# Hybrid decoder layer on one core: head transfers issued by ScalarE, no filler products among the first transposes, and two scans tied behind low parts

## The chip, the cores and the metric

The kernel runs on one core of one Trainium2 chip. The core has five engines that run side by side and meet at semaphores: TensorE (PE in the profile, with PEld for its weight loads), VectorE (DVE), ScalarE (ACT), GpSimd (POOL) and SyncE (SP), which here only issues transfers. The metric is the device time of one execution in microseconds (us); lower is better. Three runs of the kernel before gave 948.83, 948.57 and 948.82 us, median 948.82 us.

## The reference

One decoder layer works on 1024 tokens of width 1024, ahead of which 16 learned meta tokens are put, so 1040 rows:

```
u = rmsnorm(h, g_pre_mix)
q, k, v, xr, yr = split(u @ w_in)
attn = sliding_window_attention_with_sinks(q, k, v, sinks)
xr = causal_depthwise_conv(xr, conv_w, conv_b)
hr = rg_lru(xr, w_a, b_a, w_x, b_x, lambda)      # h[t] = a[t]*h[t-1] + u[t]
rec = gelu(yr) * hr
h = h + rmsnorm(concat(attn, rec) @ w_out, g_post_mix)
u = rmsnorm(h, g_pre_ffn)
h = h + rmsnorm(relu(u @ w_ff1)**2 @ w_ff2, g_post_ffn)
```

Everything is float32. The output is the last 1024 rows.

## The kernel before, in words

Every float32 operand of a large product is split into a high part (a copy rounded to fp32r, made by ScalarE) and a low part (the operand minus the high part, made by VectorE). A product is then three matmuls, high by high (line 125), high by low (line 130) and low by high (line 131); the function `mm3` issues them. So each operand has two producers, and TensorE needs both. A matmul that finds its low part unfinished stops TensorE, which takes its instructions in order.

The kernel is written in a framework that plans the order. The program text gives each instruction a priority by its place; the planner then runs a simulated timeline with its own costs and puts the instructions of each engine into one fixed queue. On the chip each engine works through its queue strictly in order, waiting where an input is not there. The text can force an order within an engine with `behind(name, ins)`, which makes no semaphore and only tells the planner that `ins` stands after `name`. `chained(0, ins)` and `chained(1, ins)` use the same means to string the instructions of ScalarE and of VectorE behind each other in the head.

**The head** (lines 138 to 530). SP issues the meta tokens (line 142), the first two tiles of 128 input rows (`load_x`, line 147), the two norm weights `g_pre_mix` and `g_pre_ffn` (lines 155, 156) and then the weights of k, v and q, the other row tiles between them (`fetch`, line 384). The norm weights land in 16 rows of `vmt`, are turned by a TensorE transpose (line 160) into the bank `pg` and copied to `gcol` (line 161), one column for each of eight groups of 128 features.

TensorE meanwhile multiplies zeros by zeros (`load`, line 309): 12 products of 512 columns and 6 of 256 stand in front of its first real work. They write a bank that nobody reads.

The first three row tiles are normed at once: meta by `norm_rows` (Square on ScalarE at line 254, the root on GpSimd at lines 170 and 176, the scaling on VectorE at line 260), the first two full tiles by `norm_first` (Square on ScalarE at line 237, for the first tile half of it on VectorE at line 242; root on ScalarE at line 82; reciprocal on VectorE at line 199; scaling in two halves at line 248). Then `transposed` turns the eight groups kc of 128 features: for each kc three transposes, of meta, tile 0 and tile 1, into one of six banks (line 358), one product of zeros behind them (line 365), the scaling by `gcol` with rounding on ScalarE (line 117) and the low part on VectorE (line 118). Two casts that make the high part of the key weight (line 344) go between the first scalings of ScalarE. The products of k and v (line 282, function `part`) start on the scaled groups. The remaining rows follow in three more pieces, each with transposes and products.

**The recurrent stage** (lines 798 to 981). The recurrent width of 512 is four chunks c of 128. For each chunk, after the gates, `decay(c)` makes the decay factor and a tanh on ScalarE, and `recur(c)` a square root on ScalarE and three VectorE instructions: lines 871 and 872, which make the input of the recurrence, and line 873, `tensor_tensor_scan`, which runs it over 1040 steps. `rec_out(c, half)` multiplies the result by the gelu branch (line 878) and splits it.

**The output projection.** `w_out` comes in eight groups kc of 128 rows. `load_wo` and `split_wo` bring and split them; their low parts are line 99 with output tag `a`, from a buffer `raw` or `d`. Groups 0 to 3 belong to the attention half; 4 and 5 meet chunks 0 and 1 of the recurrence, 6 and 7 chunks 2 and 3. `out_mm` takes groups 0 to 3 for the first four row tiles (banks pt, o, acc, s), then groups 4 and 5 for all four, then 6 and 7. The rest of the kernel, from about 260 us on, is the feed-forward part.

Of the kernel before, what the change touches and what calls it, by code (L numbers as in the profile page):

```python
# [10 lines left out]
F32R = mybir.dt.float32r  # L11
AF = mybir.ActivationFunctionType
ALU = mybir.AluOpType
# [3 lines left out]
P = 128  # L17
# [3 lines left out]
NMETA = 16  # L21
# [16 lines left out]
def hybrid_layer(  # L38
# [6 lines left out]
    nc = tc.nc  # L45
# [33 lines left out]
    last_lut = [None]  # L79
# [58 lines left out]
    ident = const.tile([P, P], F32, name="ident")  # L138
    make_identity(nc, ident)

    meta_t = slot("d", [NMETA, D])
    nc.sync.dma_start(meta_t, meta_tokens)
    xt = []

    def load_x(i):
# [6 lines left out]

    vmt = const.tile([P, P], F32, name="vmt")
    g_r = vmt[0:16, :]
    nc.sync.dma_start(g_r[0:8, :], g_pre_mix.rearrange("o (k p) -> (o k) p", p=P))
    nc.sync.dma_start(g_r[8:16, :], g_pre_ffn.rearrange("o (k p) -> (o k) p", p=P))

    gcol = const.tile([P, 16], F32, name="gcol")
    pg = bank("o")
    nc.tensor.transpose(pg[:, :16], g_r, ident[:16, :16])  # L160
    nc.vector.tensor_copy(gcol, pg[:, :16])
    g_mix_col, g_ffn_col = gcol[:, 0:8], gcol[:, 8:16]

    half_pow = const.tile([P, 1], F32, name="half_pow")
# [19 lines left out]
    eps_col = const.tile([P, 1], F32, name="eps_col")  # L184
# [7 lines left out]

    load_root()

    def root_rstd(ssq, bias, n=P):
        sd = small.tile([P, 1], F32, name="sd", tag="sd")
        lut(sd[:n], ssq, AF.Sqrt, bias=bias)
        rs = small.tile([P, 1], F32, name="rs", tag="rs")
        nc.vector.reciprocal(rs[:n], sd[:n])
        return rs[:n]  # L200


# [29 lines left out]
    def norm_first(src, halves):  # L232

        xn = slot("d", [P, D])
        ss = [small.tile([P, 1], F32, name=f"hq{i}", tag=f"hq{i}") for i in range(2)]
        c = slice(0, 512 if halves else D)
        nc.scalar.activation(
            xn[:, c], src[:, c], AF.Square, scale=RMS_SC, accum_out=ss[0]
        )
        if halves:  # L240
            c = slice(512, D)
            nc.vector.tensor_tensor_reduce(
                out=xn[:, c], in0=src[:, c], in1=src[:, c], scale=RMS_SC * RMS_SC,
                scalar=EPS, op0=ALU.mult, op1=ALU.add, accum_out=ss[1],
            )
        rs = root_rstd(ss[0], ss[1] if halves else eps_col)
        for c in (slice(0, 512), slice(512, D)):
            nc.vector.tensor_scalar(xn[:, c], src[:, c], rs, None, op0=ALU.mult)
        return xn

    def norm_rows(src, n, link=False):
        xn = slot("d", [P, D])
        ssq = small.tile([P, 1], F32, name="ssq", tag="ssq")
        ins = nc.scalar.activation(
            xn[:n], src, AF.Square, scale=RMS_SC, accum_out=ssq[:n]
        ).ins
        if link:
            chained(0, ins)
        rs = rstd_of([ssq[:n]], n)
        ins = nc.vector.tensor_scalar(xn[:n], src, rs, None, op0=ALU.mult).ins  # L260
        if link:
            chained(1, ins)
        return xn
# [35 lines left out]

    zeros = slot("ws", [P, 512], F32R)  # L300
    nc.vector.memset(f32(zeros), 0.0)

    flip = [0]

# [2 lines left out]
    def load(n, cols, after=None):  # L307
        for _ in range(n):
            ins = nc.tensor.matmul(
                idle[:, :cols], zeros[:, :P], zeros[:, :cols], start=True, stop=True,  # L310
                skip_group_check=True,
            ).ins
            if after:
                behind(after, ins)
        return ins.name

    load(12, 512)
    load(6, 256)

    def normed(b):  # L320
        if b == 0:
            return [
                (norm_rows(meta_t[:NMETA], NMETA), NMETA),
                (norm_first(xt[0], True), P), (norm_first(xt[1], False), P),
            ]
        rows = [(xt[2 * b], P), (xt[2 * b + 1], P)]
        return [(norm_rows(s[:m], m), m) for s, m in rows]


    last = [None, None]  # L330
# [1 line left out]
    def chained(e, ins):  # L332
        if last[e] is not None:
            behind(last[e], ins)
        last[e] = ins.name
# [15 lines left out]
    def transposed(b, xn, after=None):  # L351
        t0, n = ALL[b]
        for kc in range(KC):
            flip[0] += 1
            pt = bank(("pt", "o", "s")[flip[0] % 3])
            o = 0
            for s, m in xn:
                ins = nc.tensor.transpose(
                    pt[:, o : o + m], s[:m, kc * P : (kc + 1) * P], ident[:m, :m]
                )  # L360
                if after:
                    behind(after, ins.ins)
                o += m
            if b == 0:
                load(1, P, ins.ins.name)
            uh, ul = u[kc]
            if b == 0 and kc in (0, 1):
                key_casts.pop(0)()
            high = split_scaled(
                uh[:, t0 : t0 + n], ul[:, t0 : t0 + n], pt[:, :n],  # L370
                g_mix_col[:, kc : kc + 1],
            )
            if b == 0:
                chained(0, high[0])
                chained(1, high[1])
# [17 lines left out]
    xn = normed(0)  # L393
# [14 lines left out]
    low_w(wv, rv)  # L408
    wq = high_w(rq)
    low_w(wq, rq)  # L410
    km = slot("ws", [P, 4, 2 * P], F32R)
    nc.gpsimd.memset(f32(km[:, 0:2, 0 : P - NMETA]), 0.0)
    nc.gpsimd.memset(f32(km[:, 2:4, :]), 0.0)
    nsink = const.tile([P, 8], F32, name="nsink")
    nc.sync.dma_start(nsink, attn_sinks[0].partition_broadcast(P))
    prm_r = slot("d", [8, 512])
# [82 lines left out]
    for b in range(4):  # L499
# [3 lines left out]
        if b == 0:  # L503
# [5 lines left out]
            xn = [(norm_rows(xt[2], P, True), P)]  # L509
# [21 lines left out]
    for h in range(2):  # L531
        r, o, m = HALF[h], HALF[1 - h], slice(P - NMETA, 2 * P)
# [276 lines left out]
    rg = [None] * NLRU  # L809
# [48 lines left out]
    av = [None] * NLRU  # L858

    def decay(c, after=None):  # L860
        r = rg[c][0]
        av[c] = slot("b", [P, TT])
        lut(av[c], r, AF.Exp, scale=m8sp[:, c : c + 1])
        ins = lut(r, r, AF.Tanh, scale=m4sp[:, c : c + 1])
        if after:
            behind(after, ins)

    def recur(c):
        r, gi = rg[c]
        lut(r, r, AF.Sqrt, scale=-1.0)  # L870
        nc.vector.scalar_tensor_tensor(r, av[c], 1.0, r, op0=ALU.add, op1=ALU.mult)
        nc.vector.tensor_tensor(gi, gi, r, op=ALU.mult)
        nc.vector.tensor_tensor_scan(r, av[c], gi, 0.0, op0=ALU.mult, op1=ALU.add)

    def rec_out(c, half, eng=None):
        o = 512 * half
# [23 lines left out]
    def split_wo(kc, tag, eng=None):  # L900
        wo[kc] = pair(tag, [P, D])
        split(wo[kc][0], wo[kc][1], wo_raw[kc], eng)
# [45 lines left out]
        decay(c)  # L948
    for c in (0, 1):
        recur(c)  # L950
    load_wo(0, "raw")
    load_wo(1, "raw")
    load_wo(2, "d")
# [3 lines left out]
    for kc in range(1, 4):  # L957
        split_wo(kc, "a")
        wo_cast[kc] = cast[0]
    decay(2, wo_cast[1])  # L960
    decay(3, wo_cast[2])
    for c in (2, 3):
        recur(c)
    for half in range(2):
        for c in range(NLRU):
            y = ys[c][:, 512 * half : 512 * half + 512]
            ins = lut(y, y, AF.Gelu_apprx_tanh)
            if half == 0 and c == 0:
                behind(wo_cast[3], ins)
    for c0 in (0, 2):  # L970
        at[0][2 + c0 // 2] = pair("b", [P, 2, 512])
        for c in (c0, c0 + 1):
            rec_out(c, 0)
            rec_low = mark[0]
        for kc in range(4 + c0, 6 + c0):
            load_wo(kc, ("d", "raw")[kc % 2])
            split_wo(kc, "a")
    for cp in (2, 3):
        at[1][cp] = pair("b", [P, 2, 512])
    for c in range(NLRU):  # L980
# [487 lines left out]
    halves = {}  # L1468
# [159 lines left out]
```

## Time and profile before

| what | us |
|---|---|
| median of three runs | 948.82 |
| the profiled execution | 949.06 |
| its span, first to last instruction | 947.4 |
| PE busy | 936.9 |
| DVE busy | 664.3 |
| ACT busy | 504.3 |
| POOL busy | 133.9 |

A row of the timeline gives the start in us from the span's start, the duration, the engine, the line of the kernel, the operation, what it writes and reads with shapes, how many such instructions were merged, and in brackets how long the engine had stood idle and what released it. SPq, ACTq and POOLq are the queues of those engines that issue transfers. Matmuls overlap, so a matmul's duration is longer than its distance to the next one; the distance of starts is the cost in a full queue.

### The profile page before, as it was taken

What the parts mean: (1) busy time and instruction counts of PE and PEld (TensorE: products, weight loads), DVE (VectorE), ACT (ScalarE), POOL (GpSimd) and SP (SyncE); (2) the same over time, 40 slices, a digit from 0 to 9 for tenths busy, and PEclk for the clock granted to TensorE, in tenths of its full rate; (3) what the DMA queues carried; (4) which work ended last, traced back from release to release, by engine and by line L of the source; (5) the groups of instructions that cost most, each with busy time, mean ns of one, the idle gap of its engine ahead of it and who ended that gap; (6) DMA issues with size and microseconds to landing.
All of it is one profiled execution on the core that took longest, in us unless ns stands there. A gap on an engine that the chain in (4) does not pass through costs nothing.

```text
span 947.4 us, 12177 instructions
## 1 busy us (share of the span) xinstructions
PE 936.9 (99%) x4584; PEld 783.6 (83%) x4584; DVE 664.3 (70%) x848; ACT 504.3 (53%) x845; POOL 133.9 (14%) x205
## 2 busy tenths in 40 slices
PE   9999999999999999999999999999999999999996
PEld 8999999877788878888888888888888888888885
DVE  6667788889877987665544465476667676779883
ACT  8546765679434664443655575654533443445441
POOL 4104436430021200010000000001111000001201
PEclk9999999999999999999999999999999999999999
DMA  8220011104359659574422364334877756637924
GB/s 273 57 66 25 24 46 45 45 23 140 102 176 271 200 182 285 187 256 134 156 89 89 111 214 121 108 112 112 199 168 176 211 178 194 186 131 209 239 63 89
DMA packets 97366, 134.91 MB, mean 142 GB/s; under 512 B 22230, under 2 KB 61158, under 8 KB 97308
## 3 DMA queue, kind: packets, MB, share of 16 engines
q1 hardware_dynamic: 87996, 108.64, 36.2%
q0 software_dynamic: 8880, 24.19, 12.2%
q10 hardware_dynamic: 432, 1.31, 0.4%
q8 instruction: 36, 0.59, 0.3%
q14 instruction: 22, 0.18, 0.1%
HBM read 112.55 MB, written 20.97 MB: 141 GB/s over the span
## 4 chain that ended last, share of the span: by engine, by line
PE 94%; DVE 3%; issue 1%; DMA 1%; ACT 0%; DVEq 0%; SPq 0%
PE ps_acc L125 11%; PE ps_acc L131 11%; PE ps_acc L130 11%; PE ps_pt L131 6%; PE ps_pt L130 6%; PE ps_pt L125 6%; PE ps_s L125 6%; PE ps_s L131 6%; PE ps_s L130 6%; PE ps_o L125 5%; PE ps_o L130 5%; PE ps_o L131 5%; PE ps_o L699 2%; PE ps_acc L917 1%; PE ps_acc L282 1%
## 5 line engine op out<-in xcount | busy, mean ns | idle before, releaser
L99 DVE TENSOR_TENSOR ws<-raw,ws 128x1024 fp32r<-128x1024 f32 (+1 forms) x69 | 83.1, 1204 | 69.9 <-PE ps_o L130 23.0
L96 ACT CAST ws<-raw 128x1024 fp32r<-128x1024 f32 (+1 forms) x68 | 69.8, 1027 | 82.3 <-PE ps_o L130 33.1
L96 ACT CAST ws<-e 128x1024 fp32r<-128x1024 f32 x41 | 43.0, 1049 | 85.5 <-PE ps_o L130 38.3
L99 DVE TENSOR_TENSOR b<-b,b 128x1024 fp32r<-128x1024 f32 (+1 forms) x49 | 57.5, 1176 | 27.8 <-PE ps_o L130 22.5
L130 PE MATMUL ps_acc<-a,ws 128*128 128x512 f32 (+3 forms) x224 | 76.3, 341 | 0.0
L125 PE MATMUL ps_acc<-a,ws 128*128 128x512 f32 (+3 forms) x224 | 76.3, 341 | 0.0
L131 PE MATMUL ps_acc<-a,ws 128*128 128x512 f32 (+3 forms) x224 | 75.7, 338 | 0.0
L99 DVE TENSOR_TENSOR ws<-e,ws 128x1024 fp32r<-128x1024 f32 x41 | 50.1, 1222 | 31.8 <-ACT ws L96 18.5
L96 ACT CAST b<-b 128x1024 fp32r<-128x1024 f32 (+1 forms) x49 | 49.5, 1011 | 41.7 <-DVE b L1096 35.6
L686 POOL TENSOR_SCALAR_AFFINE_SELECT c<-c 128x512 fp32r<-128x512 f32 x64 | 53.2, 846 | 73.6 <-ACT c L96 64.6
L131 PE MATMUL ps_acc<-ws,b 128*128 128x512 f32 (+1 forms) x120 | 46.1, 384 | 0.0
L130 PE MATMUL ps_acc<-ws,b 128*128 128x512 f32 (+1 forms) x120 | 46.1, 384 | 0.0
L125 PE MATMUL ps_acc<-ws,b 128*128 128x512 f32 (+1 forms) x120 | 46.0, 385 | 0.0
L125 PEld LDWEIGHTS ps_acc<-a,ws 128*128 128x128 f32 x224 | 42.2, 188 | 3.1 <-DVE b L926 0.3
L131 PEld LDWEIGHTS ps_acc<-a,ws 128*128 128x128 f32 x224 | 42.2, 188 | 3.0
L130 PEld LDWEIGHTS ps_acc<-a,ws 128*128 128x128 f32 x224 | 42.1, 188 | 2.8
L125 PE MATMUL ps_pt<-ws,b 128*128 128x512 f32 x112 | 44.3, 395 | 0.0
L130 PE MATMUL ps_pt<-ws,b 128*128 128x512 f32 x112 | 44.2, 395 | 0.0
L131 PE MATMUL ps_pt<-ws,b 128*128 128x512 f32 x112 | 44.0, 392 | 0.0
L125 PE MATMUL ps_s<-ws,b 128*128 128x512 f32 x110 | 43.4, 395 | 0.0
L130 PE MATMUL ps_s<-ws,b 128*128 128x512 f32 x110 | 43.3, 393 | 0.0
L131 PE MATMUL ps_s<-ws,b 128*128 128x512 f32 x110 | 43.2, 393 | 0.0
(421 smaller groups left out, 2682.3 us busy)
## 6 DMA issues: line engine op xcount, KB each, us to landing
raw<-in_w_ff_dram SPq DMA_DIRECT2D x59, 512.0 KB, 3.8
e<-in_w_ff_dram SPq DMA_DIRECT2D x43, 512.0 KB, 3.5
a<-in_w_ff_dram SPq DMA_DIRECT2D x12, 512.0 KB, 6.2
s_dram<-a POOLq DMA_DIRECT2D x12, 512.0 KB, 3.8
raw<-in_w_in_dram SPq DMA_DIRECT2D x9, 512.0 KB, 3.7
c<-in_x_dram SPq DMA_DIRECT2D x8, 512.0 KB, 5.1
d<-in_x_dram SPq DMA_DIRECT2D x8, 512.0 KB, 3.4
out_dram<-raw SPq DMA_DIRECT2D x8, 512.0 KB
```

The lines of the kernel that those rows point to most:

```text
L96: cast[0] = nc.scalar.copy(hi, src).ins.name
L99: low = nc.vector.tensor_tensor(lo, src, f32(hi), op=ALU.subtract).ins
L125: ins = nc.tensor.matmul(dst, lh, rh, start=start, stop=False, skip_group_check=True).ins
L130: nc.tensor.matmul(dst, lh, rl, start=False, stop=False, skip_group_check=True)
L131: last_mm[0] = nc.tensor.matmul(dst, ll, rh, start=False, stop=stop, skip_group_check=True).ins.name
L282: last_mm[0] = nc.tensor.matmul(acc[:, :n], w[k // 2][:, kc, :], u[kc][k % 2][:, t0 : t0 + n], start=k == 0 and kc == 0, stop=k == last an ...
L686: nc.gpsimd.affine_select(out=p_[:, :, s], in_=f32(p_[:, :, 0]), pattern=[[0, 4], [g, P]], compare_op=op, fill=0.0, base=0, channel_multip ...
L699: nc.tensor.matmul(two[:, :, oc : oc + w], v, p_.rearrange("p (j i) s c -> p j (i s c)", j=2)[:, :, pc : pc + w], start=n == 0 and k == 0, ...
L917: ins = nc.tensor.matmul(y2_bank[half], (wh, wh, wl)[k][:, kc, :], (uh, ul, uh)[k][:, t0 : t0 + n], start=m % 24 == 0, stop=m % 24 == 23, ...
```

## The change

1. The issue of the meta tokens and of the two norm weights moves from SP to ScalarE.
2. The transpose of the norm weights moves from the head of TensorE's queue to between the products of zeros: 8 products of 512 columns, the transpose, 4 more of 512 and 4 of 256 (before: 12 of 512 and 6 of 256). Its copy to `gcol` moves into `norm_first` of the first tile, ahead of the reciprocal.
3. The eight products of zeros among the first transposes go away.
4. Orders are tied: the Square of tile 1 behind the last ScalarE table function, its reciprocal behind the scaling of tile 0, and the norms of the third piece into the chains of ScalarE and VectorE.
5. The second cast of the key weight moves from group 1 to group 2 of the features.
6. The zeros for the key block of the meta tokens (`km`) are written in the text before the first transposes.
7. The scan leaves `recur` and becomes a function of its own. The scan of chunk 0 follows both `recur(0)` and `recur(1)`; that of chunk 1 is tied behind the low part of group 2 of `w_out`; that of chunk 2 follows both `recur(2)` and `recur(3)`; that of chunk 3 is tied behind the low part of group 5 of `w_out` and that of `rec_out(1, 0)`.

```
-    nc.sync.dma_start(meta_t, meta_tokens)
+    nc.scalar.dma_start(meta_t, meta_tokens)
...
-    nc.sync.dma_start(g_r[0:8, :], g_pre_mix.rearrange("o (k p) -> (o k) p", p=P))
-    nc.sync.dma_start(g_r[8:16, :], g_pre_ffn.rearrange("o (k p) -> (o k) p", p=P))
+    nc.scalar.dma_start(g_r[0:8, :], g_pre_mix.rearrange("o (k p) -> (o k) p", p=P))
+    nc.scalar.dma_start(g_r[8:16, :], g_pre_ffn.rearrange("o (k p) -> (o k) p", p=P))
...
-    pg = bank("o")
-    nc.tensor.transpose(pg[:, :16], g_r, ident[:16, :16])
-    nc.vector.tensor_copy(gcol, pg[:, :16])
...
-        nc.vector.reciprocal(rs[:n], sd[:n])
+        ins = nc.vector.reciprocal(rs[:n], sd[:n]).ins
+        if after:
+            behind(after, ins)
...
+        if not halves:
+            behind(last_lut[0], square)
...
+            nc.vector.tensor_copy(gcol, pg[:, :16])
+        rs = root_rstd(ss[0], ss[1] if halves else eps_col, after=scaled[0])
...
+    km = slot("ws", [P, 4, 2 * P], F32R)
+    nc.gpsimd.memset(f32(km[:, 0:2, 0 : P - NMETA]), 0.0)
+    nc.gpsimd.memset(f32(km[:, 2:4, :]), 0.0)
...
-    load(12, 512)
-    load(6, 256)
+    pg = bank("o")
+    turned = nc.tensor.transpose(pg[:, :16], g_r, ident[:16, :16]).ins
+    behind(load(8, 512), turned)
+    load(4, 512, turned.name)
+    load(4, 256)
...
-        return [(norm_rows(s[:m], m), m) for s, m in rows]
+        return [(norm_rows(s[:m], m, b == 2), m) for s, m in rows]
...
-            if b == 0:
-                load(1, P, ins.ins.name)
...
-            if b == 0 and kc in (0, 1):
+            if b == 0 and kc in (0, 2):
...
-        nc.vector.tensor_tensor_scan(r, av[c], gi, 0.0, op0=ALU.mult, op1=ALU.add)
+
+    def scan(c, *after):
+        r, gi = rg[c]
+        ins = nc.vector.tensor_tensor_scan(
+            r, av[c], gi, 0.0, op0=ALU.mult, op1=ALU.add
+        ).ins
+        for name in after:
+            behind(name, ins)
...
     for c in (0, 1):
         recur(c)
+    scan(0)
...
         split_wo(kc, "a")
         wo_cast[kc] = cast[0]
+        if kc == 2:
+            scan(1, mark[0])
...
     for c in (2, 3):
         recur(c)
+    scan(2)
...
+        if c0 == 0:
+            scan(3, mark[0], rec_low)
```

More of the change, by code (lines that the diff above doesn't have):

```diff
@@ L193, in hybrid_layer, with root_rstd @@
     load_root()
-    def root_rstd(ssq, bias, n=P):
+    def root_rstd(ssq, bias, n=P, after=None):
         sd = small.tile([P, 1], F32, name="sd", tag="sd")
@@ L236, in norm_first @@
         c = slice(0, 512 if halves else D)
-        nc.scalar.activation(
+        square = nc.scalar.activation(
             xn[:, c], src[:, c], AF.Square, scale=RMS_SC, accum_out=ss[0]
-        )
+        ).ins
+        if not halves:
+            behind(last_lut[0], square)
         if halves:
@@ L245, in norm_first @@
             )
-        rs = root_rstd(ss[0], ss[1] if halves else eps_col)
+            nc.vector.tensor_copy(gcol, pg[:, :16])
+        rs = root_rstd(ss[0], ss[1] if halves else eps_col, after=scaled[0])
         for c in (slice(0, 512), slice(512, D)):
-            nc.vector.tensor_scalar(xn[:, c], src[:, c], rs, None, op0=ALU.mult)
+            scaled[0] = nc.vector.tensor_scalar(
+                xn[:, c], src[:, c], rs, None, op0=ALU.mult
+            ).ins.name
         return xn
+    scaled = [None]
     def norm_rows(src, n, link=False):
@@ L410, in hybrid_layer @@
     low_w(wq, rq)
-    km = slot("ws", [P, 4, 2 * P], F32R)
-    nc.gpsimd.memset(f32(km[:, 0:2, 0 : P - NMETA]), 0.0)
-    nc.gpsimd.memset(f32(km[:, 2:4, :]), 0.0)
     nsink = const.tile([P, 8], F32, name="nsink")
@@ L872, in recur @@
         nc.vector.tensor_tensor(gi, gi, r, op=ALU.mult)
-        nc.vector.tensor_tensor_scan(r, av[c], gi, 0.0, op0=ALU.mult, op1=ALU.add)
+    def scan(c, *after):
+        r, gi = rg[c]
+        ins = nc.vector.tensor_tensor_scan(
+            r, av[c], gi, 0.0, op0=ALU.mult, op1=ALU.add
+        ).ins
+        for name in after:
+            behind(name, ins)
     def rec_out(c, half, eng=None):
```

## The prediction

> **What bounds the kernel now.** I read the page first, for the busy shares and the chain that ended last, then the waits of TensorE, then the timeline at the two places that the change touches: the first 13 us and the stretch from 226 to 258 us.
>
> ```profile
> PE 936.9 (99%) x4584; PEld 783.6 (83%) x4584; DVE 664.3 (70%) x848; ACT 504.3 (53%) x845; POOL 133.9 (14%) x205
> ...
> PE 94%; DVE 3%; issue 1%; DMA 1%; ACT 0%; DVEq 0%; SPq 0%
> ```
>
> ```profile
> PE ps_o L358 <- DVE d L248: 0.6, 1, 0.6
> PE ps_pt L130 <- DVE a L99: 0.5, 2, 0.3
> ```
>
> The reader should see that TensorE is the bound: 99% busy, 94% of the chain. A change that removes no real product can only win where TensorE waits, and the view of its waits names two such places beside its start: a wait for the scaled tile 1 in the head, and two waits for low parts of `w_out`. The change aims at both. Whatever TensorE saves there moves everything behind it forward, since no other wait of TensorE stands in that view.
>
> **Part 1: the head (transfers, norm weights, zeros).** First the chain of waits, then rows of the timeline.
>
> ```profile
> 1.71 4.89 DMA c<-in_x_dram
> 6.62 1.16 ACT d L237 x2
> ...
> 8.13 0.17 DVE rs L199
> 8.33 0.79 DVE d L248
> ```
>
> ```profile
> 0.80 0.40 SPq L142 DMA_DIRECT2D d<-in_meta_tokens_dram  x1
> 1.26 0.88 SPq L147 DMA_DIRECT2D c<-in_x_dram  x2
> ```
>
> ```profile
> 0.80 1.28 ACT L82 ACT_TABLE_LOAD   x1 [0.80 <-PEq L1612]
> 2.92 1.06 ACT L254 ACTIVATE d<-d 16x1024 f32<-16x1024 f32 x1 [0.63 <-DMA d<-in_meta_tokens_dram]
> ...
> 9.68 0.49 ACT L117 ACTIVATE a<-ps_o,gcol 128x272 fp32r<-128x272 f32 x1 [1.07 <-DVE gcol L161]
> ...
> 12.80 0.53 ACT L117 ACTIVATE a<-ps_s,gcol 128x272 fp32r<-128x272 f32 x1
> ```
>
> The end of the head is set by one path: tile 1 lands at 6.60 (1.71 + 4.89), then Square, root, reciprocal, scaling, the transposes, and from 9.68 to 13.33 ScalarE scales the eight groups without a pause. Only then can TensorE run its products without holes.
>
> SP issues meta at 0.80 and the two row tiles from 1.26. With meta on ScalarE, the tiles are issued from 0.80, 0.46 earlier. I let tile 1 land 0.46 earlier too. The bounds: 0 if the transfers limit each other (meta's 64 KB then run beside tile 0 and not ahead of it), and 0.46 as the issue row has it. I take 0.46, the row nearest to it: the landing follows the issue by 4.89 us, far more than the issue itself.
>
> The price is on ScalarE. Three issues stand ahead of its table load. At 0.40 each, the row of the same transfer on SP, the load starts 1.2 later, at 2.0, and ends at 3.28; the small root behind it takes 0.2, so meta's Square starts at about 3.5 and not 2.92, 0.58 late. What is behind meta is GpSimd's root and VectorE's scaling of meta:
>
> ```profile
> 5.91 0.74 DVE L260 TENSOR_SCALAR d<-d,rs 16x1024 f32<-16x1024 f32 x1
> 6.57 0.14 DVE L199 RECIPROCAL rs<-sd 128x1 f32<-128x1 f32 x1
> 6.75 0.88 DVE L248 TENSOR_SCALAR d<-c,rs 128x512 f32<-128x512 f32 x2
> ```
>
> Meta's scaling stands in VectorE's queue ahead of the reciprocal of tile 0. Even if it stays at 5.91, the scaling of tile 0 ends at 7.63 as now, and the reciprocal of tile 1, now at 8.13, is wanted at 8.13 - 0.46 = 7.67. So the lateness of meta is just covered, by 0.04 us; beyond that each tenth costs a tenth, up to the whole 0.46. The copy of the norm weights, tied into that queue before the reciprocal, adds its 0.16 only if TensorE has turned them late. It has not: eight products of zeros end near 5 us.
>
> The order ties (tile 1's Square and reciprocal) repeat the order of the queues above and cost nothing. The copy to `gcol` was what released ScalarE at 9.68; now it is done near 5.5, but the transposes of tile 1 end at the same time, so it alone frees no more than 0.1, which I count as nothing. The second key cast moves one group back within ScalarE's unbroken row from 9.68 to 13.33: sum unchanged, 0.
>
> The zeros:
>
> ```profile
> 1.51:6.34 4.83, 4.83 (x11) 3.80 (x12) 1.00 0.86 270
> ```
>
> ```profile
> L309 PE MATMUL ps_acc<-ws 128*128 128x128 f32 x8 | 1.8, 299 | 0.0
> ```
>
> The first row (a window on the products of zeros alone) has 11 products of 512 columns in 4.83 us, 0.44 each, against 0.23 later (rows below). So TensorE is slow until about 6.3, though the granted clock reads 1.00. Sixteen products are left of eighteen, so they still end near 7.1, ahead of the first transposes. The second row has the eight that go: 1.8 us of busy time, all in a stretch where ScalarE's scaling decides. I cost their removal at 0. The bounds are a gain of 1.8 if TensorE and not ScalarE were the limit there, and a loss if TensorE falls back to half rate (a rival below).
>
> Two edits with one answer: the zeros of `km` and the tied norms of the third piece.
>
> ```profile
> 8.31 0.53 POOL L413 MEMSET ws<- 128x512 f32 x1
> ```
>
> ```profile
> 19.15 1.07 ACT L254 ACTIVATE d<-c 128x1024 f32<-128x1024 f32 x1
> ```
>
> ```profile
> 32.12 0.27 PE L358 MATMUL ps_s<-ident,d 128*128 128x128 f32 x1
> ```
>
> The memsets need a place ahead of meta's GpSimd step; at most the 0.53 and its shorter neighbour could delay it, which is in the 0 to 0.46 above. The Square of row tile 4 goes behind a cast, some 2 us later; its transposes come at 32.12, more than 8 us on. Both 0.
>
> Head: 0.46 gained, bounds 0 and 0.46.
>
> **Part 2: the scans.** VectorE first, then TensorE.
>
> ```profile
> 226.58:257.30 30.72, 30.63 (x32) 1.00 0.28 91
> ```
>
> ```profile
> 226.58 4.53 DVE L873 TENSOR_TENSOR_SCAN c<-b,c 128x1040 f32<-128x1040 f32 x2
> 231.03 1.20 DVE L99 TENSOR_TENSOR a<-d,a 128x1024 fp32r<-128x1024 f32 x1
> ...
> 233.90 1.22 DVE L99 TENSOR_TENSOR a<-raw,a 128x1024 fp32r<-128x1024 f32 x1
> ...
> 243.65 2.31 DVE L873 TENSOR_TENSOR_SCAN c<-b,b 128x1040 f32<-128x1040 f32 x1
> 245.89 1.20 DVE L99 TENSOR_TENSOR a<-raw,a 128x1024 fp32r<-128x1024 f32 x1
> 247.00 0.68 DVE L99 TENSOR_TENSOR b<-b,b 128x512 fp32r<-128x512 f32 x1
> ...
> 251.85 0.69 DVE L99 TENSOR_TENSOR b<-d,b 128x512 fp32r<-128x512 f32 x1
> ```
>
> ```profile
> 231.68 0.40 PE L131 MATMUL ps_s<-ws,b 128*128 128x512 f32 x1
> 232.28 0.50 PE L130 MATMUL ps_pt<-a,b 128*128 128x512 f32 x1 [0.21 <-DVE a L99]
> ...
> 235.14 0.40 PE L130 MATMUL ps_acc<-a,b 128*128 128x512 f32 x1
> 235.37 0.39 PE L130 MATMUL ps_pt<-a,b 128*128 128x512 f32 x1
> ```
>
> ```profile
> 246.44 0.40 PE L125 MATMUL ps_pt<-a,b 128*128 128x512 f32 x1
> 247.14 0.51 PE L130 MATMUL ps_pt<-a,b 128*128 128x512 f32 x1 [0.30 <-DVE a L99]
> 247.74 0.50 PE L131 MATMUL ps_pt<-a,b 128*128 128x512 f32 x1
> ```
>
> ```profile
> 257.79 0.39 PE L125 MATMUL ps_pt<-a,b 128*128 128x512 f32 x1
> ```
>
> VectorE is never idle in these 31 us, so a swap of two of its instructions moves work and removes none. TensorE's step in a full queue is 0.23 (235.14 to 235.37). At 232.28 it stands 0.60 after its forerunner, 0.37 lost, and 0.11 more on the next product: it waited for the low part of group 2, which stood behind both scans. With scan 1 behind that low part, the low part ends at about 228.9 + 1.2 = 230.1, well ahead, and the 0.48 is saved. But the low part of group 3 (233.90, done at 235.12) is wanted by the product at 235.37, which now comes at 234.89: the wait that is late next. If VectorE's queue is otherwise as now, 0.28 and some 0.10 of restart come back and 0.10 is gained; if the planner, with group 2 ready early, puts other products there, 0.48. Neither row is nearer; I take the middle, 0.29.
>
> At 247.14 and 247.74 the steps are 0.70 and 0.60, 0.47 and 0.37 lost, and 0.10 after them: 0.94. They waited for the low parts of group 5 and of chunk 1, behind scan 3. With scan 3 behind both, they end at about 244.8 and 245.4, ahead of 246.4: 0.94 gained. Scan 3 then ends where the second low part ended, near 247.7, and the rest of VectorE's queue is where it was. Its reader, chunk 3, is split by 252.5, and groups 6 and 7 are wanted at 257.79: 5.3 us of cover, against 1.7 that TensorE gains. Scan 1 ends 1.2 later; its reader stands more than 5 us behind it in the same queue. Nothing else is queued on VectorE behind a new wait, because the ties make no semaphore.
>
> Scans: 1.23 gained, bounds 1.04 and 1.42.
>
> **The sum.** 0.46 + 1.23 = 1.69. The profiled execution took 949.06, so it would take 947.37. It was 0.24 slower than the median of the runs, 948.82; against that I forecast 947.1.
>
> **Rivals.**
>
> *TensorE falls back to half rate (slower).* Between the last zeros near 7.1 and the first full stretch of products, at 12.1 after the shift, TensorE does transposes, holes and a few products; the eight zeros stood in those holes. For it: the slow start above shows that TensorE must be kept at work before it runs at full rate. Against it: the stretch without zeros between 7.4 and 9.3 did not slow it. Price: slow as long as at the start, 4.83 us from the first product, at 0.44 for 0.23: 4.83 x (1 - 0.23/0.44) = 2.3. With the 1.69 that gives 949.4; the point from which it decides is 3.5 us of slow products, and two such stretches give 951.7.
> The Trainium skill, "TensorE: Matmul & The Clock Gate", Part 4, says that transposes do not count as work for that gate, and Part 1 that an idle window of about 3.4 us halves the rate; by it alone the stretch from 7.1 to the first products would just be long enough. The trace agrees with the slow start; a fall-back is in no row here.
>
> *The planner gives the freed place on VectorE to other work (slower or same).* Each instruction of 1.2 put ahead of a low part that TensorE wants costs 1.2, a scan 2.31. From two such on, the gain is gone: 948.8 + 2.31 - 1.69 + 1.2 = 950.6 with both. For it: the queue has no hole. Against it: the ties name just these low parts.
>
> *The waits only move.* The scans' gain is taken back by the next low part; the head alone is left: 948.4.
>
> *The head gains nothing.* Meta on ScalarE is late, or the tiles land no sooner: 948.8 - 1.23 = 947.6.
>
> *More than forecast.* If TensorE limits the transposes, up to half of the 1.8 us of zeros is gained too: 946.2.
>
> **How the numbers follow.** Both places gain as summed: 0.56. The clock rival 0.10, the planner 0.10, waits that move 0.08, no head 0.07, more 0.09. About 0.2%, 1.9 us, is what a measurement of this kernel can tell from no change; the line lies at 946.9, so close to the forecast that the first case splits, 0.27 beyond and 0.29 short. Faster: 0.27 + 0.09 = 0.36. Slower: the planner's 0.10 and 0.07 of the clock's: 0.17. The rest, 0.47, is the same. The range goes from 946.2 to 949.4; 0.17 above and little below are left out. The forecast's own range is 946.9 to 947.8 (sums of 1.88 and 1.04).
>
> **What would show it.** In the profile after: Square of tile 1 near 6.2 and the first scaling by `gcol` near 9.2; the wait on L248 gone or earlier; products of k dense from about 12.9 with unchanged steps. Scan 1 behind the low part of group 2, no step above 0.35 around 232 and 247. Wrong would be the forecast if the Square of tile 1 stays at 6.6, if matmuls of 272 columns after 12 us take twice their step, or if a wait on a low part of `w_out` is found in another place.

## The result, and the profile after

| | before | after |
|---|---|---|
| median of 21 runs each, us | 948.76 (948.41 to 949.63) | 950.41 (949.80 to 951.22) |
| ratio after to before | | 1.0016, 95% interval 1.0010 to 1.0022 |
| profiled execution, us | 949.06 | 950.34 |
| its span, us | 947.4 | 948.6 |

The changed kernel is 1.65 us slower. The forecast was 947.1 with a range from 946.2 to 949.4, so it missed by 3.3 us and on the other side of no change; the loss is still within 0.2%.

To see where it sits, I take one and the same product of TensorE, counted from the end of its queue, and compare when it starts in the two traces.

| product, from the end | start before, us | shift after, us |
|---|---|---|
| 4500th | 16.73 | +1.18 |
| 4200th | 52.02 | +2.27 |
| 3300th | 197.06 | +2.34 |
| 3000th | 259.64 | +1.33 |
| last | 939.46 | +1.37 |

The scan stage, between the third and the fourth row, gives 1.0 back, where 1.23 was forecast. But 1.18 is lost in the first 17 us, where 0.46 was to be gained, and another 1.1 in the next stretch. These two losses were not in the sum.

The busy shares of the page after, with TensorE at 99% as before, and then the view of TensorE's waits (what waited, for whom; us in total, times, longest):

```profile
PE 937.9 (99%) x4574; PEld 783.5 (83%) x4574; DVE 663.6 (70%) x848; ACT 504.2 (53%) x845; POOL 135.0 (14%) x205
```

```profile
PE ps_o L328 <- POOL rs L173: 0.9, 1, 0.9
PE ps_pt L371 <- DVE a L118: 0.6, 1, 0.6
```

Both waits aimed at are gone, the one on the scaled tile 1 and the two on `w_out`. Two others stand in their place: L328 is the transpose of the norm weights, L371 is a transpose of the second piece. For the first the view names GpSimd's root, which came last there; runs e6 and e7 below show that the landing of the norm weights ends this wait.

**The first new wait.** Rows of the timeline after, first 11 us:

```profile
0.80 0.42 ACTq L142 DMA_DIRECT2D d<-in_meta_tokens_dram  x1
1.25 0.57 ACTq L155 DMA_DIRECT2D vmt<-in_g_pre_mix_dram  x1
1.84 0.28 ACTq L156 DMA_DIRECT2D vmt<-in_g_pre_ffn_dram  x1
2.16 1.28 ACT L82 ACT_TABLE_LOAD   x1 [2.16 <-issue]
...
5.96 1.06 ACT L236 ACTIVATE d<-c 128x1024 f32<-128x1024 f32 x1 [0.19 <-DMA c<-in_x_dram]
...
10.86 0.49 ACT L117 ACTIVATE a<-ps_o,gcol 128x272 fp32r<-128x272 f32 x1 [2.91 <-PE ps_o L371]
```

```profile
1.51 3.78 PE L319 MATMUL ps_acc<-ws 128*128 128x512 f32 x8 [1.51 <-DVE base_e L571]
6.16 0.26 PE L328 MATMUL ps_o<-ident,vmt 16*128 16x16 f32 x1 [0.86 <-POOL rs L173]
6.34 2.93 PE L319 MATMUL ps_acc<-ws 128*128 128x512 f32 x8
9.20 0.28 PE L371 MATMUL ps_o<-ident,d 16*128 16x16 f32 x1
```

Tile 1 is there 0.66 us earlier (its Square at 5.96, before 6.62). Yet the first scaling comes at 10.86, before 9.68. TensorE finishes its first eight products of zeros at 5.29, stands until 6.16 for the transpose, and then takes 2.93 us for the eight products of zeros behind it (four of 512 columns, four of 256). At 0.23 for 512 columns they would take about 1.4; at 0.44, the slow rate of the start, 2.6. So TensorE had not left the slow rate, and the first transposes of rows start at 9.20 where they started at 7.40. In the kernel before, the planner had put the transpose of the norm weights among those:

```profile
7.40 0.23 PE L358 MATMUL ps_s<-ident,d 16*128 16x16 f32 x1
...
7.67 0.21 PE L160 MATMUL ps_o<-ident,vmt 16*128 16x16 f32 x1
```

**The second new wait.** Row tile 4 belongs to the third piece, and its scaling is line 260 before and 267 after. First before, then after, with the low parts (118) of the second piece behind it:

```profile
23.07 0.75 DVE L260 TENSOR_SCALAR d<-c,rs 128x1024 f32<-128x1024 f32 x1
...
24.74 0.48 DVE L118 SCALAR_TENSOR_TENSOR a<-ps_pt,gcol,a 128x256 fp32r<-128x256 f32 x1
```

```profile
23.32 1.96 POOL L627 COPY c<-nsink 128x2 f32<-128x2 f32 x8 [0.79 <-DVE nsink L553]
25.37 0.22 POOL L167 TENSOR_SCALAR ms<-ssq 128x1 f32<-128x1 f32 x1
...
26.28 0.75 DVE L267 TENSOR_SCALAR d<-c,rs 128x1024 f32<-128x1024 f32 x1 [1.01 <-POOL rs L173]
27.07 0.48 DVE L118 SCALAR_TENSOR_TENSOR a<-ps_pt,gcol,a 128x256 fp32r<-128x256 f32 x1
...
27.61 0.44 PE L371 MATMUL ps_pt<-ident,d 128*128 128x128 f32 x2 [0.58 <-DVE a L118]
```

Before, this scaling ran at once. After, its Square is tied behind a cast and its root stands behind eight copies on GpSimd; VectorE waits 1.01 us for it, and all low parts of the second piece, which need nothing of tile 4, wait behind it. The transpose at 27.61 then waits for a bank that a low part has still to read.

**The scans**, VectorE and TensorE after:

```profile
231.15 1.20 DVE L99 TENSOR_TENSOR a<-d,a 128x1024 fp32r<-128x1024 f32 x1
232.27 2.32 DVE L884 TENSOR_TENSOR_SCAN c<-b,c 128x1040 f32<-128x1040 f32 x1
...
245.98 1.22 DVE L99 TENSOR_TENSOR a<-raw,a 128x1024 fp32r<-128x1024 f32 x1
247.12 0.68 DVE L99 TENSOR_TENSOR b<-b,b 128x512 fp32r<-128x512 f32 x1
247.72 2.31 DVE L884 TENSOR_TENSOR_SCAN c<-b,b 128x1040 f32<-128x1040 f32 x1
```

```profile
233.96 0.40 PE L131 MATMUL ps_o<-a,b 128*128 128x512 f32 x1
234.33 0.73 PE L125 MATMUL ps_pt<-a,b 128*128 128x512 f32 x2
...
247.78 0.39 PE L131 MATMUL ps_s<-a,b 128*128 128x512 f32 x1
248.01 0.39 PE L125 MATMUL ps_pt<-a,b 128*128 128x512 f32 x1
```

The scans of chunks 1 (232.27) and 3 (247.72) stand behind the low parts as tied. Around 247 all steps are 0.23; the largest one left in this stage is 0.37, at 234.33.

### The profile page after: what moved, and what is told of

Read it like the earlier page. It is cut to its first block, busy times and chain, and to the rows that moved or that the text cites. A ratio compares the mean times of both kernels' runs of the same rounds, so it can differ in the third digit from the quotient of the medians.

```text
span 948.6 us, 12157 instructions
## 1 busy us (share of the span) xinstructions
PE 937.9 (99%) x4574; PEld 783.5 (83%) x4574; DVE 663.6 (70%) x848; ACT 504.2 (53%) x845; POOL 135.0 (14%) x205
## 3 DMA queue, kind: packets, MB, share of 16 engines
q10 hardware_dynamic: 496, 1.38, 0.4%
## 4 chain that ended last, share of the span: by engine, by line
PE 97%; DVE 1%; POOL 0%; DMA 0%; issue 0%; ACT 0%; DVEq 0%
PE ps_acc L131 11%; PE ps_acc L125 11%; PE ps_acc L130 11%; PE ps_pt L130 6%; PE ps_pt L125 6%; PE ps_s L131 6%; PE ps_s L125 6%; PE ps_pt L131 6%; PE ps_s L130 6%; PE ps_o L125 5%; PE ps_o L130 5%; PE ps_o L131 5%; PE ps_o L707 2%; PE ps_acc L932 1%; PE ps_s L637 1%; PE ps_s L641 1%
```

## The experiments

Each kernel ran 11 times (e7: 6), beside the kernel before on the same chip. In the first four the kernel before had a median of 948.87, in e6, e7, e8 and e10 948.70, in the last four 948.88. These groups ran on three different chips, so kernels of different groups are compared by the third column; the kernel after stands at +1.65.

| kernel | median, us | difference to before on the same chip, us | ratio to before, 95% interval |
|---|---|---|---|
| e1 turn back | 947.70 | -1.17 | 0.9989 (0.9980 to 0.9998) |
| e2 no link | 950.01 | +1.14 | 1.0010 (1.0001 to 1.0019) |
| e3 both back | 948.10 | -0.77 | 0.9992 (0.9983 to 1.0000) |
| e4 scans only | 947.84 | -1.03 | 0.9990 (0.9981 to 0.9998) |
| e6 no zeros behind the turn | 948.50 | -0.20 | 0.9998 (0.9988 to 1.0007) |
| e7 norm weights first | 951.67 | +2.97 | 1.0032 (1.0020 to 1.0043) |
| e8 = e1, tile 4 behind low parts | 947.23 | -1.47 | 0.9984 (0.9975 to 0.9993) |
| e10 = after, tile 4 behind low parts | 949.41 | +0.71 | 1.0008 (0.9999 to 1.0017) |
| e9 = e1 with zeros among transposes | 947.74 | -1.14 | 0.9986 (0.9977 to 0.9995) |
| e11 twelve products in front | 947.99 | -0.89 | 0.9990 (0.9981 to 0.9998) |
| e12 = e1 with SP's issues | 948.23 | -0.65 | 0.9993 (0.9984 to 1.0002) |
| e13 = e11, tile 4 behind low parts | 947.47 | -1.41 | 0.9988 (0.9979 to 0.9997) |

### Which part costs: e1, e2, e3, e4

e1 puts the transpose of the norm weights, its copy and all 18 products of zeros back as they were; ScalarE's issues, the ties and the scans stay.

```
+    pg = bank("o")
+    nc.tensor.transpose(pg[:, :16], g_r, ident[:16, :16])
+    nc.vector.tensor_copy(gcol, pg[:, :16])
...
-    pg = bank("o")
-    turned = nc.tensor.transpose(pg[:, :16], g_r, ident[:16, :16]).ins
-    behind(load(8, 512), turned)
-    load(4, 512, turned.name)
-    load(4, 256)
+    load(12, 512)
+    load(6, 256)
```

> The changed kernel with the transpose of the norm weights, its copy and the zeros ahead of it where they were before (12 products of 512 and 6 of 256, then the transpose); issue from ScalarE, the link of the norms and the scans stay as changed. Theory (in the changed kernel the transpose waits on TensorE for the norm weights, 0.9 us, and the eight products of zeros tied behind it then run at half rate and keep the first transposes back until 9.2): TensorE is fed from near 9.2 by ScalarE again, the head goes from 1.2 us later than before to about 0.5 earlier, total 950.4 - 1.7 = 948.7. Rival (the missing eight zeros among the transposes cost the head): the head stays 1.2 late, total 950.4.

It takes 947.70, better than the theory gave. Its timeline:

```profile
1.51 5.91 PE L321 MATMUL ps_acc<-ws 128*128 128x512 f32 x18 [1.51 <-DVE base_e L570]
...
6.02 1.06 ACT L239 ACTIVATE d<-c 128x1024 f32<-128x1024 f32 x1 [0.17 <-DMA c<-in_x_dram]
7.36 0.23 PE L160 MATMUL ps_o<-ident,vmt 16*128 16x16 f32 x1
9.11 0.49 ACT L117 ACTIVATE a<-ps_o,gcol 128x272 fp32r<-128x272 f32 x1 [1.10 <-PE ps_s L370]
...
23.03 0.78 DVE L269 TENSOR_SCALAR d<-c,rs 128x1024 f32<-128x1024 f32 x1 [0.29 <-POOL rs L176]
```

TensorE runs 18 products of zeros in one piece, and the first scaling comes at 9.11, 0.57 ahead of before. So the head does gain, and the turned position hid it; what the gain is made of follows under e12. The shift of the 4500th product goes from +1.18 to -0.57. By the 4200th it is only -0.10: the scaling of tile 4 still waits here, for 0.29.

e2 takes the tie of the third piece away from the kernel after.

```
-        return [(norm_rows(s[:m], m, b == 2), m) for s, m in rows]
+        return [(norm_rows(s[:m], m), m) for s, m in rows]
```

> The changed kernel without the tie of the third piece's norms into the chains of ScalarE and VectorE. Theory (the scaling of row tile 4 stands in VectorE's queue ahead of the low parts of the second piece and waits 1.0 us for its root): the wait at 26.3 on VectorE and the one at 27.6 on TensorE go, total 950.4 - 1.06 = 949.3. Rival (these waits follow from the late head alone): they stay, 950.4.

The theory fell: 950.01 (its eleven runs spread from 948.75 to 950.90, too wide to tell it from the kernel after), and 0.88 of TensorE's time still goes between the 4500th and the 4200th product. Without the tie the planner puts the scaling of tile 4 even further forward, ahead of the low parts of k, and it waits there (timeline of e2, VectorE):

```profile
22.40 0.75 DVE L267 TENSOR_SCALAR d<-c,rs 128x1024 f32<-128x1024 f32 x1 [0.76 <-POOL rs L173]
```

So not the tie as such, but where this scaling stands in VectorE's queue, became the next theory.

e3 makes both edits at once.

> Both of the above at once: norm weights turned as before and no tie of the third piece's norms. What is left of the change: issue from ScalarE, no zeros among the transposes, scans. Theory: the sum of the two, 948.7 - 1.06 = 947.6, and if the head gains all of its 0.66 us of earlier landing 947.2, faster than the kernel before. Rival (the missing zeros cost): 949.3 or more.

948.10, 0.4 above e1: with the early head the tie seems to help a little. The scaling of tile 4 stands at 20.74, again ahead of the low parts of k and with a wait of 0.76, and TensorE loses 0.70 between the 4500th and the 4200th product, against 0.47 in e1.

e4 is the kernel before with only the scans moved, as in part 7 of the change.

```
-        nc.vector.tensor_tensor_scan(r, av[c], gi, 0.0, op0=ALU.mult, op1=ALU.add)
+
+    def scan(c, *after):
...
+    scan(0)
...
+            scan(1, mark[0])
...
+    scan(2)
...
+            scan(3, mark[0], rec_low)
```

> The kernel before with the scans moved and nothing else. Theory: 1.0 us gained between 226 and 258 us and nothing elsewhere, 948.76 - 1.0 = 947.75; no step of TensorE above 0.35 us near 247. Rival (the gain there is only the late head's slack): no gain, 948.8.

947.84, that is 1.03 below the kernel before; in the trace the shift falls by 1.01 between the 3300th and the 3000th product. The part of the scans stands by itself. The head of e4 is that of the kernel before, and yet the 4500th product comes 0.48 later in its trace than in the trace before. So a shift in the head, read from one trace each, can be off by half a microsecond.

### What keeps the transpose waiting, and what the wait spoils: e6, e7, e11

e6 leaves out the eight products of zeros behind the transpose (nobody reads them).

```
     behind(load(8, 512), turned)
-    load(4, 512, turned.name)
-    load(4, 256)
```

> The changed kernel without the eight products of zeros tied behind the transposed norm weights (eight are left in front of it). Theory (the head is late because those eight run at the slow rate, 0.43 us each, after TensorE stood waiting for the norm weights): the first transposes start near 7.4 and not at 9.20, the first scaling by gcol near 9.2 and not at 10.86, and about 1.2 us or more of the head comes back: 949.2 or less. Rival (these products keep TensorE's clock up, and without them the first real products are slow): the first scaling is as early, but the products of k after 12 us take about 0.4 per 512 columns, and the total is 950.4 or more.

The timeline of e6, TensorE and the first scaling:

```profile
6.22 0.25 PE L328 MATMUL ps_o<-ident,vmt 16*128 16x16 f32 x1 [0.92 <-DMA vmt<-in_g_pre_ffn_dram]
7.18 0.28 PE L369 MATMUL ps_o<-ident,d 16*128 16x16 f32 x1 [0.71 <-DVE d L267]
...
8.20 0.42 PE L369 MATMUL ps_s<-ident,d 128*128 128x128 f32 x1
8.41 0.42 PE L369 MATMUL ps_pt<-ident,d 128*128 128x128 f32 x1
...
9.72 0.49 ACT L117 ACTIVATE a<-ps_o,gcol 128x272 fp32r<-128x272 f32 x1 [1.53 <-PE ps_o L369]
```

948.50, 1.9 below the kernel after. The transposes start at 7.18, as the theory had it; the first scaling comes at 9.72, later than its 9.2 and near before's 9.68. The rival was right on the rate: the transposes come every 0.21, where e1's come every 0.11, so TensorE stays slow, in this trace until 13.50. In the first 17 us that cost less than the zeros did, the shift there being +0.19. Here the trace names the landing of the norm weights as what ended the wait, where the kernel after had GpSimd's root.

e7 issues the norm weights ahead of the meta tokens.

```
+    nc.scalar.dma_start(g_r[0:8, :], g_pre_mix.rearrange("o (k p) -> (o k) p", p=P))
+    nc.scalar.dma_start(g_r[8:16, :], g_pre_ffn.rearrange("o (k p) -> (o k) p", p=P))
     nc.scalar.dma_start(meta_t, meta_tokens)
```

> The changed kernel with the two norm weights issued by ScalarE ahead of the meta tokens, about 0.4 us earlier. Theory (the transpose of the norm weights stands in TensorE's queue and waits for their landing, and each tenth that they land earlier is a tenth less of idle TensorE): the transpose starts at about 5.7, the zeros behind it end near 8.8, the first scaling comes near 10.4, total 950.0; and if the hole falls below what breaks the start of TensorE, the zeros run at full rate, the first scaling comes near 9.2 and the total is near 949. Rival (GpSimd's root of the meta tokens, which the waits name, releases the transpose): it starts at 6.16 or later, since meta now comes later, total 950.4 or more.

The timeline of e7:

```profile
1.72 0.40 ACTq L146 DMA_DIRECT2D d<-in_meta_tokens_dram  x1
...
5.23 0.28 PE L328 MATMUL ps_o<-ident,vmt 16*128 16x16 f32 x1
5.44 1.73 PE L319 MATMUL ps_acc<-ws 128*128 128x512 f32 x8
...
7.19 1.05 ACT L261 ACTIVATE d<-d 16x1024 f32<-16x1024 f32 x1 [3.54 <-DMA d<-in_meta_tokens_dram]
...
10.14 0.23 PE L371 MATMUL ps_o<-ident,d 16*128 16x16 f32 x1 [2.98 <-DVE d L267]
```

This settles the cause of the wait and misses the total. The transpose runs at 5.23 without any wait, although meta and its root are later than ever: it is the landing of the norm weights that it waits for, not GpSimd. And without the hole the same eight products behind it take 1.73 us where the kernel after needs 2.93: the hole had cost the full rate. But the meta tokens, now issued third, land 5.5 us after their issue, and everything waits for them until 10.14. The total is 951.67, the slowest of all. Not all of that is meta's: five of the six runs also have a granted clock of 0.994 to 0.996 and take 951.49 to 952.73, the sixth has 0.998 and takes 950.37. The last section shows where the clock went.

e11 changes the kernel after in one number and its complement: twelve products of 512 in front of the transpose, four of 256 behind.

```
-    behind(load(8, 512), turned)
-    load(4, 512, turned.name)
-    load(4, 256)
+    behind(load(12, 512), turned)
+    load(4, 256, turned.name)
```

> The changed kernel with twelve products of zeros of 512 columns in front of the turned norm weights where it has eight, and the four of 256 behind; sixteen in all, as in the changed kernel. Theory (only the idle stretch that the wait for the norm weights opens does the harm): the twelve end near 6.6, after the norm weights land near 6.1, TensorE has no hole, the first scaling by gcol comes near 9.2, and the time is that of the kernel with the transpose put back, 947.7. Rival (the tied place of the transpose or of its copy costs by itself): the first scaling stays later than 9.9, 949 or more.

The timeline of e11:

```profile
6.93 0.28 PE L328 MATMUL ps_o<-ident,vmt 16*128 16x16 f32 x1
7.15 0.91 PE L319 MATMUL ps_acc<-ws 128*128 128x256 f32 x4
7.99 0.23 PE L370 MATMUL ps_o<-ident,d 16*128 16x16 f32 x1
...
9.73 0.49 ACT L117 ACTIVATE a<-ps_o,gcol 128x272 fp32r<-128x272 f32 x1 [1.70 <-PE ps_o L370]
```

947.99: 2.5 us come back, with the same edits and the same number of products. The wait is gone, so neither the tied place of the transpose nor its copy is the harm. The profiled scaling at 9.73 is later than expected, since the zeros last until 7.99. Against e1 0.28 is missing; the repaired pair e13 and e8 differs by only 0.06, so this remainder stays open.

### What the tie of tile 4 costs: e10, e8, e13

All three put the scaling of row tile 4 behind all low parts of the second piece in VectorE's queue; nothing else is moved.

```
-        return [(norm_rows(s[:m], m, b == 2), m) for s, m in rows]
+        return [(norm_rows(s[:m], m, ["low", True][i] if b == 2 else False), m)
+                for i, (s, m) in enumerate(rows)]
...
-        if link:
+        if link == "low":
+            behind(low_u[0], ins)
+        elif link:
             chained(1, ins)
...
+            low_u[0] = high[1].name if b == 1 else low_u[0]
```

> The changed kernel with the scaling of row tile 4 put behind all low parts of the second piece in VectorE's queue, nothing else moved. Theory (the scaling, which waits for its root behind GpSimd's copies, costs the 1.06 us between 23 and 31 us): TensorE's waits for banks at 27.61 and 30.15 go, total 949.4. Rival (the loss there only follows from the late head, and moves to another wait): 950.4.

> The kernel with the transpose of the norm weights put back in front (947.7), and the scaling of row tile 4 put behind all low parts of the second piece in VectorE's queue; nothing else moves. Theory (this scaling waits for its root and holds up the first low parts of the second piece): the 0.45 us that TensorE gave back between 22 and 33 us are kept, total 947.3, the best so far. Rival (they are lost to something else, or row tile 4 is now late for its own transposes near 31 us): 947.7 or more.

> Twelve products of zeros in front of the turned norm weights, and the scaling of row tile 4 behind the low parts of the second piece. Theory: both repairs add, 947.2, as the version with the transpose put back in front and the same scaling moved. Rival (with the transpose tied in the middle, the second repair has nothing to recover): 947.7.

In the kernel after (e10) it brings 0.94: 949.41. On top of e1 (e8) it brings 0.30: 947.23, the fastest kernel here, 1.47 below the kernel before. On top of e11 (e13) it brings 0.52 by the medians, 947.47, but four of the eleven runs of e13 took 948.8, so that this one is not secured. VectorE in e8:

```profile
23.79 0.48 DVE L118 SCALAR_TENSOR_TENSOR a<-ps_pt,gcol,a 128x256 fp32r<-128x256 f32 x1
...
28.78 1.41 DVE L269 TENSOR_SCALAR d<-c,rs 128x1024 f32<-128x1024 f32 x2
```

The low parts start at 23.79 (24.73 in e1), and tile 4 is scaled at 28.78 without a wait. In e10 the shift is +1.46 at the 4500th product and +1.38 at the 4200th: the second loss is gone while the first one stands. They are two causes.

### The terms taken as nothing, and the issue: e9, e12

e9 puts the eight products among the first transposes back into e1.

```
+            if b == 0:
+                load(1, P, ins.ins.name)
```

> The kernel with the transpose of the norm weights put back in front (947.7), and also the eight products of zeros among the first transposes put back. Theory (ScalarE's scaling sets the pace there, the products cost and give nothing): 947.7. Rival (TensorE is the limit among the transposes): up to 1.8 us slower, 949.5. Third (they keep TensorE at full rate): under 947.2.

947.74 against 947.70: they cost and give nothing.

e12 gives the three issues of e1 back to SP.

> The kernel with the transpose of the norm weights put back in front (947.7), and the three head transfers issued by SP again. Theory (the row tiles land some 0.5 us earlier because SP has one issue fewer ahead of them, and that is the whole gain of the head): Square of tile 1 back near 6.6, the first scaling near 9.7, total 948.2. Rival (the gain of the head comes from the missing products of zeros or from chance): 947.7, no change.

ScalarE in the timeline of e12:

```profile
6.57 1.06 ACT L239 ACTIVATE d<-c 128x1024 f32<-128x1024 f32 x1 [0.28 <-DMA c<-in_x_dram]
```

948.23: 0.52 is lost, and the Square of tile 1 is back at 6.57. That is the worth of ScalarE's issues in the total. But the first scaling moves less than the Square: 9.34 here against 9.11 in e1, only 0.23. Rows of VectorE, first the kernel before, then after, tell why:

```profile
8.33 1.17 DVE L248 TENSOR_SCALAR d<-c,rs 128x512 f32<-128x512 f32 x2
```

```profile
6.13 0.74 DVE L267 TENSOR_SCALAR d<-d,rs 16x1024 f32<-16x1024 f32 x1 [0.77 <-POOL rs L173]
...
7.96 0.88 DVE L250 TENSOR_SCALAR d<-c,rs 128x512 f32<-128x512 f32 x2
```

With ScalarE's issues the scaling of meta waits 0.77 for GpSimd's root (it starts at 6.13 in after, 6.21 in e1, 5.82 in e12), and the scaling of tile 1, behind it in the queue, starts at 7.96, 8.05 and 8.28. About half of what the Square gains is lost there. And that scaling takes 1.17 in the kernel before, while GpSimd writes the zeros of `km` beside it (8.09 to 8.84), but 0.88 or 0.89 in every kernel here with the changed head, where these zeros are done at 4.04. So by the traces some 0.3 of the head's gain is due to the zeros of `km`; no run moves them alone.

## Why the prediction was wrong

**The head: the step that failed.** The norm weights were to be turned in time, because (on turning them late) "It has not: eight products of zeros end near 5 us." This took TensorE's own queue as the only thing that sets when the norm weights are turned. The products did end at 5.29. But the transpose also needs the norm weights, which are issued at 1.25 and 1.84 and land only around 6.1; I had counted ScalarE's issues as a delay of ScalarE alone and never asked when what they issue lands. In the kernel before the transpose stood at 7.67, where any landing was early enough, so its trace showed no wait. The sentence "Sixteen products are left of eighteen, so they still end near 7.1", fell with it: the hole kept TensorE slow (2.93 us for eight products, 1.73 without a hole), and they ended at 9.2. With the turned position undone, the kernel gains 2.8 us (from +1.65 to -1.17 against the kernel before).

**The earlier tile: the size came out, the working only in part.** Forecast 0.46; tile 1's Square came 0.66 earlier, and e1 against e12 measures 0.52. But "So the lateness of meta is just covered, by 0.04 us" did not hold. The table load came at 2.16 (forecast 2.0), meta's Square at 3.69 (3.5), and the first GpSimd step behind it took 0.51 where it takes 0.23 in the kernel before. So the root came late for VectorE, and the scaling of tile 1 started only 0.37 earlier (8.33 to 7.96), in e1 0.28. Another 0.3 came from the zeros of `km`, costed at 0. That the head's total is near the forecast is therefore partly luck.

**The third piece: the second failed step.** "The Square of row tile 4 goes behind a cast, some 2 us later; its transposes come at 32.12, more than 8 us on. Both 0." named the wrong cover. What stands next behind that scaling is not its own reader but the low parts of the second piece, in the same queue. Worth 0.9 in the kernel after (e10), 0.3 with an early head (e8).

**The zeros among the transposes** were rightly counted as nothing (e9). The second key cast was not tried alone.

**The scans were right in their mechanism**: 1.0 (e4: 1.03) where 1.23 was forecast, just under the lower bound of 1.04. The term of 0.94 at 247 is there in full. The 0.29 at 232 was too much: steps of 0.37, 0.34, 0.28 and 0.34 remain around 234 and 237. Against 0.23 each they lose 0.41 of the 0.48 again, the wait that is late next.

With the measured terms the sum goes from before to after: the head's gain 0.4 (e8 against e4), scans 1.0 gained, the second loss 0.9. From the measured +1.65 the turned position is then left with 1.65 + 0.4 + 1.0 - 0.9 = 2.15; that is a remainder, and the 2.8 of e1 has about 0.6 of the second loss in it (in the traces, 1.1 lost between the 4500th and the 4200th product after, 0.47 in e1).

**The rivals.** None names the mechanism. "TensorE falls back to half rate" came closest, 949.4 from slow products after 12 us, but TensorE did not fall back: it had not got up, and what it did slowly were the zeros. All 21 runs of the kernel after have a granted clock of 0.997 or 0.998, where the runs with a fall-back (last section) have 0.994 to 0.996. "The planner" put work ahead of a low part, but in the second piece, not in the scan stage.

## What to carry to other kernels

Before an instruction is moved forward in a queue that works in order, list every input it has and when each one lands: a wait that never showed in the old place tells nothing of the new one. The cover of an instruction that is made later is not when its own result is read, but what stands right behind it in its engine's queue. And filler work that is meant to bring an engine up to rate must not have a wait in its middle.

## What was not expected of the hardware

**A short hole delayed the full rate by one whole step.** By the trace's clock record TensorE is at full rate from 6.34 us in the kernel before, and from 4.67 to 7.61 in the kernels here whose zeros ran without a hole in front of the turn. With a hole of 0.7 to 1.0 us it is 9.63 (after), 9.87 (e2) and 10.12 (e10), and 13.50 in e6, which has a hole and no zeros behind it. The granted clock of the windows reads 1.00 even before that, so the steps of the zeros must be read. The half rate of e7 below lasts 6.83 us by the same record; if that is two steps, one is 3.41. One step ahead of its raise the kernel after is at 6.22, and of the step that ends there TensorE stands idle from 5.29 to 6.16, a quarter; it is busy for 75%, in e2 for 78%, in e10 for 71%. In the step that brought the raise it was busy for 92% or more in every trace. The Trainium skill, "TensorE: Matmul & The Clock Gate", Part 1, says that the window of activity runs freely, about 3.4 us long. The spread of the starts without a hole (2.9 us) and the delay by about 3.5 us (median 6.3 without a hole, 9.9 in after, e2 and e10) agree.

**The fall-back that was a rival happened in e7.** TensorE idles from 7.17 to 10.14, then does transposes alone. The windows of e7 (columns: stretch, then busy time and count of PE, PEld, DVE, ACT and POOL, granted clock, DMA share, GB/s):

```profile
12.80:19.60 6.80, 6.80 (x29) 6.07 (x30) 6.43 (x11) 6.80 (x13) 0.72 (x1) 0.52 1.03 307
19.60:30.00 10.40, 10.40 (x91) 10.40 (x89) 7.79 (x16) 6.62 (x18) 6.63 (x17) 1.00 0.75 221
```

The granted clock is 0.52 for 6.8 us, right when the first real products come: 29 of them where the next 10.4 us have 91. So the rival's mechanism exists; the change itself did not reach it. By the granted clock it came in six of the eleven runs of e6 too: they have 0.995 and take 948.50 to 949.37, the other five have 0.997 or 0.998 and take 947.87 to 948.18. The Trainium skill, same page, Part 4, says that transposes do not count as work for that gate; the half rate that follows 2.4 us of transposes alone (10.14 to 12.5) agrees, though TensorE had also stood idle for 3 us before them.

**Order of issue counted for more than size.** The meta tokens issued first, at 0.80, are read at 3.69; issued third, at 1.72 and behind the row tiles that SP had issued, they are there at 7.19. The 8 KB of norm weights land some 4.2 us after the second issue when they are behind meta (1.84 to about 6.1), and at most 3.8 when they are first (1.42 to 5.23).

**VectorE and GpSimd were slower beside each other.** Beside GpSimd's zeros for `km` the two halves of VectorE's scaling of tile 1 take 0.78 and 0.47 in the kernel before, and 0.81 and 0.82 in e4, where the larger of GpSimd's two writes lasts 0.80 and not 0.53; alone they take 0.48 or 0.49 (after, e1, e12). The other way round, the GpSimd step behind meta's Square takes 0.23 in the kernel before, e4, e7 and e12. In after, e1 and e6 it starts during VectorE's half Square of tile 0 and takes 0.51, 0.53 and 0.73; it ends 0.09 after that Square each time.
